# Where a loop's exponentials and gate products are queued

## The chip, the cores and the metric

The kernel runs on one core of a Trainium2 chip. The metric is the device time of one execution in microseconds; times inside an execution are counted from the start of the profiled span. The engines are named as the profile names them: PE (TensorE matmul), PEld (its weight loads), DVE (VectorE), ACT (ScalarE), POOL (GpSimd), SP (SyncE, which here only issues transfers). Each works through its own queue in order.

## The reference

One layer over 512 tokens of width 1024: a gated spatial mix and a banded attention, both projected and added to the input, and then a feed-forward part with 16384 experts, which is where the change lies. Cut to that part:

```python
def block(xb):                                   # 128 tokens
    q = (xb @ w_query).reshape(128, 8, 2, 128)   # 8 heads, 2 halves
    sc = einsum('thpd,hpkd->thpk', q, sub_keys)
    s_top, i_top = lax.top_k(sc, 16)
    cand = s_top[:, :, 0, :, None] + s_top[:, :, 1, None, :]
    cand_idx = i_top[:, :, 0, :, None] * 128 + i_top[:, :, 1, None, :]
    best, pos = lax.top_k(cand.reshape(128, 8, 256), 16)
    eidx = take_along_axis(cand_idx.reshape(128, 8, 256), pos, axis=-1)
    g = softmax(best, axis=-1)
    h = gelu(einsum('thkd,td->thk', expert_u[eidx], xb))
    return einsum('thk,thkd->td', g * h, expert_v[eidx])
```

## The kernel before, in words

The 512 tokens are four tiles of 128. For 320 tokens (and 64 further ones that are handled on the side) the expert part is computed densely: all 16384 experts in 128 tiles of 128, as `gelu(U x)` times a gate that is zero for experts that were not chosen, and then times `V`. For the first tile of 128 tokens it is computed by gathering: 16 rows of `U` and 16 of `V` for each of 8 heads.

The loop at the end of the kernel runs over 64 chunks of two expert tiles. The **first product** (PE, L194 to L196, into one of two PSUM buffers `pu`) makes `U x`; a **gelu** on ACT (L719) moves it to `act` and so frees the buffer. The **second product** (L1202) multiplies by `V` and adds to PSUM. The first products run 25 chunks ahead of the second ones (`AHEAD`): 50 gelus lie ahead of the loop, and in chunk c the loop does second product c and, while c + 25 < 64, the first products and two gelus of chunk c + 25. So the first 39 chunks hold both products and the last 25 only the second.

For each chunk the second product needs: two tiles of `V` (a transfer to `raw`, a copy to `hi` on ACT, L155, and a difference `lo`, L156, mostly on DVE); `act` times the gates `gc` (two DVE products, L1168); the copy `wh` of that on ACT (L1169) and the difference `wl` on DVE (L1170), each in one of two buffers. The gates are loaded (L1002) for groups of eight expert tiles, which is four chunks (`GB // BC`), into two buffers in turn, one group ahead.

The gathered tile's heads are **routed** in the loop, one every third chunk (`ROUTE`), by `route_gathered`: the best keys (DVE), the casts L762 and L763 (ACT), the choice (DVE, with one copy on POOL), and the **softmax**: a subtraction (L803, DVE), an exponential (L804, ACT), a sum, a reciprocal and a product (L806 to L808, DVE). Rows are then gathered by POOL; DVE multiplies each row of `U` with the tokens (L1128), ACT takes the gelu of 16 such results (L1132), DVE multiplies them with the head's softmax (L1133) and adds each row of `V` with that weight (L1139).

Only PE's order is written out by hand in the loop. The other engines' queues are ordered by a planner, which starts from the order in the program, priorities (the second products and the first products ahead have a raised one) and the times at which it expects inputs. `queued_behind(marks)` and `tc.issue_after(ins)` add one constraint: an instruction of the block that runs on the engine of `ins` comes behind `ins` in that engine's queue. It adds no wait. `done` holds the last gelu, `marked` the last `wl` difference (and, before the loop, the last instruction of that kind of work on DVE).

Of the kernel before, what the change touches and what calls it, by code (L numbers as in the profile page):

```python
# [13 lines left out]
AF = mybir.ActivationFunctionType  # L14
# [5 lines left out]
P = 128  # L20
# [7 lines left out]
TOPK = 16  # L28
# [23 lines left out]
BC = 2  # L52
# [26 lines left out]
PARTS = 8  # L79
ROUTE = 3  # L80
GB = 8
# [12 lines left out]
def hybrid_block(tc, x, ln1, w_in, gng, wsT, bsb, qkg, bias, w_out, ln2, wq, skT, uT, ud, vd, out):  # L94
    nc = tc.nc
    ctx = ExitStack()
    with ctx:
# [28 lines left out]
        def queued_behind(marks):  # L126

            ctx = ExitStack()
            for i in marks:
                ctx.enter_context(tc.issue_after(i))  # L130
            return ctx
# [557 lines left out]
        begun, more, done, behind, routed = [], [], [], [], []  # L689
# [51 lines left out]
        def keys(pool, n):  # L741

            return (pool.tile([P, 2, n, 2, TOPK], F32, name="top", tag="top", bufs=2),
                    pool.tile([P, n, 2, TOPK], U32, name="pos", tag="pos", bufs=2))

        def best_keys(pool, top, pos, u, p2, src):
            rep = pool.tile([P, NK], F32, name="rep", tag="rep", bufs=2)
            return top16(top[:, 0, u, p2, :], pos[:, u, p2, :], src, rep)
# [47 lines left out]
                                          mask[:, i, :, :, None].to_broadcast([P, n, TOPK, m]), other)  # L796
            nc.vector.tensor_copy(to, tree[:, :, :, 0])

        def softmax(pool, best, n):

            full = [P, n, TOPK]
            ex = pool.tile(full, F32, name="ex")
            nc.vector.tensor_tensor(ex, best, best[:, :, 0:1].to_broadcast(full), op=ALU.subtract)  # L803
            nc.scalar.activation(ex, ex, AF.Exp)  # L804
            zs = pool.tile([P, n], F32, name="zs")
            nc.vector.reduce_sum(zs, ex, axis=AX.X)  # L806
            nc.vector.reciprocal(zs, zs)
            nc.vector.tensor_tensor(best, ex, zs[:, :, None].to_broadcast(full), op=ALU.mult)  # L808
# [186 lines left out]
        gcs, marked = {}, []  # L995
# [20 lines left out]
        with tc.manual_schedule(engines=engines):  # L1016
# [5 lines left out]
            for n in range(steps + LEAD):  # L1022
                t, c = divmod(n, per)
# [65 lines left out]
        ep = ctx.enter_context(tc.tile_pool(name="ep", bufs=1, reuse_waits="tile"))  # L1089
        gcp.append(ep)  # L1090

        def scores_of(b, eng):
            n = NH // PARTS
            sc = ep.tile([P, n, 2, NK], F32, name="sc0", tag="sc0", bufs=2)
            load = eng.dma_start(sc.rearrange("p h a n -> p h (a n)"),
                                 s0d[b * n:(b + 1) * n].rearrange("h p a -> p h a"))
            return sc, getattr(load, "ins", load)
# [9 lines left out]
        def route_gathered(b):  # L1107

            n = NH // PARTS
            sc = (scores.pop(b) if b in scores else scores_of(b, nc.sync))[0]  # L1110
            top, pos = keys(ep, n)
            for h in range(n):
                for p2 in range(2):
                    best_keys(ep, top, pos, h, p2, sc[:, h, p2, :])
            hs = slice(b * n * TOPK, (b + 1) * n * TOPK)
            best, to = (x[:, 0, hs].rearrange("p (h k) -> p h k", k=TOPK) for x in (gate, eidx))
            mask = ep.tile([P, 6 * n * TOPK], U32, name="mask", tag="mask", bufs=1)
            tree = ep.tile([P, D], F32, name="tree", tag="row", bufs=ROW)
            choose(ep, pairs(ep, top, pos, n, behind=list(routed if b else done)), n, best, to, mask,
                   tree[:, 0:n * TOPK * 32].rearrange("p (h k m) -> p h k m", h=n, k=TOPK))  # L1120
            softmax(ep, best, n)
            nc.vector.tensor_copy(eint[:, hs], eidx[:, 0, hs])

        def gather_u(j):
            row = ep.tile([P, D], F32, name="row", tag="row", bufs=ROW)
            nc.gpsimd.indirect_dma_start(out=row, out_offset=None, in_=ud,  # L1126
                                         in_offset=bass.IndirectOffsetOnAxis(ap=eint[:, j:j + 1], axis=0))
            nc.vector.scalar_tensor_tensor(row, row, 1.0, xb0, op0=ALU.mult, op1=ALU.mult,  # L1128
                                           accum_out=hw[:, j:j + 1])
            if j % TOPK == TOPK - 1:  # L1130
                hs = slice(j + 1 - TOPK, j + 1)
                nc.scalar.activation(hw[:, hs], hw[:, hs], AF.Gelu_apprx_tanh)  # L1132
                nc.vector.tensor_tensor(hw[:, hs], hw[:, hs], gate[:, 0, hs], op=ALU.mult)  # L1133
# [24 lines left out]
        def second_product(c, between):  # L1158
            w = weights.pop(c) if c in weights else rows_of_v(c)
            gc = gcs[c * BC // GB]  # L1160
            act = acts.pop(c)
            wh = ep.tile([P, BC, NDT], F32R, name="wh", tag="wh", bufs=2)
            wl = ep.tile([P, BC, NDT], F32R, name="wl", tag="wl", bufs=2)
            with queued_behind(marked if c < GB // BC else []):
                for b in range(BC):
                    bb = (c * BC + b) % GB
                    av = act[:, b, :].rearrange("p (n t) -> p n t", t=TG)
                    nc.vector.tensor_tensor(av, av, gc[:, 0:NDU // TG, bb, :], op=ALU.mult)  # L1168
            nc.scalar.activation(wh[:, :, 0:NDU], act, AF.Copy)  # L1169
            mark = nc.vector.tensor_tensor(wl[:, :, 0:NDU], act, wh[:, :, 0:NDU].bitcast(F32), op=ALU.subtract)  # L1170
            marked[:] = [getattr(mark, "ins", mark)]
            if c == 1:
                with tc.issue_after(loads[-1]):
                    load_gates(1, nc.sync)
            elif c * BC % GB == 0 and 0 < c * BC < NB - GB:
                load_gates(c * BC // GB + 1, nc.sync)
            b0 = (c * BC) % GB

            def last_tokens():
                gu = gc[:, NDU // TG:, b0:b0 + BC, :]  # L1180
                hu, lu = (w_[:, :, NDU:].rearrange("p b (n t) -> p n b t", t=TG) for w_ in (wh, wl))
                pair = (nc.scalar.activation(hu, gu, AF.Copy),
                        nc.vector.tensor_tensor(lu, gu, hu.bitcast(F32), op=ALU.subtract))
                own_last[:] = [getattr(i, "ins", i) for i in pair]

            if c:
                with queued_behind(own_last if c < GB // BC else []):
                    last_tokens()
            order = [(b, t) for b in range(BC) for t in range(ND)]
            if c in (0, NCHK - 1):  # L1190
                order.sort(key=lambda bt: bt[1])
            for i, (b, t) in enumerate(order):
                if c == 0 and i == BC * (ND - 1):
                    between()
                    with queued_behind(halved):
                        last_tokens()
                first = c == 0 and b == 0
                last = c == NCHK - 1 and b == BC - 1
                tok = slice(t * P, (t + 1) * P)
                def product(half, k):  # L1200
                    ds_ = slice(half * 512, (half + 1) * 512)
                    nc.tensor.matmul(accs[t][half], (wh, wh, wl)[k][:, b, tok], w[b][k % 2][:, ds_],  # L1202
                                     start=first and k == 0, stop=last and k == 2)

                if c == NCHK - 1:
                    parts = [(half, k) for half in range(2) for k in range(3)]
                else:
                    parts = [(half, k) for half in range(2) for k in range(2)] + [(0, 2), (1, 2)]
                for half, k in parts:
                    product(half, k)  # L1210
            return mark
# [3 lines left out]
        with tc.manual_schedule(engines={mybir.EngineType.PE}):  # L1215
            for c in range(NCHK):
                def ahead():
                    if c + AHEAD < NCHK:
                        for _ in first_products((c + AHEAD) * BC, BC):
                            pass  # L1220

                with tc.high_priority(offset=PRIO):
                    mark = second_product(c, ahead)
                    if c:
                        ahead()
                if c % ROUTE == 0 and c < PARTS * ROUTE:
                    route_gathered(c // ROUTE)
                passed = c + 1 + min(c + 1, NCHK - AHEAD)
                with tc.issue_after(mark.ins if hasattr(mark, "ins") else mark):
                    gather_some(min(total, total * max(0, passed - DELAY) // (weight - SLACK - DELAY))  # L1230
                                - (total - len(gathers)))
            gather_some(len(gathers))
# [53 lines left out]
```

## Time and profile before

| | |
|---|---|
| median of 3 runs | 1425.32 us (1420.27 to 1426.73) |
| the profiled execution | 1418.47 us |
| its span | 1416.7 us |
| mean granted PE clock | 0.998 |
| PE busy | 1387.3 us, 98% of the span |
| DVE busy | 1157.5 us, 82% |
| ACT busy | 610.5 us, 43% |
| POOL busy | 699.0 us, 49% |

A busy share is a mean over stages. The loop begins at about 585 us; its first 39 chunks end at about 1212 us, and a chunk there takes 15.3 us of PE, later 8.2 us. In the profile's rows an instruction has its start, its duration, engine, line, operation, and what it writes and reads; a bracket behind it gives the time its engine stood idle before it and what ended that.

### The profile page before, as it was taken

To read this page: it belongs to the slowest core of one execution; us is meant where nothing else is said; L and a number is where in the kernel's file an instruction comes from. 1 tells how busy PE (TensorE), PEld (TensorE's weight loads), DVE (VectorE), ACT (ScalarE), POOL (GpSimd) and SP (SyncE) were. 2 spreads that over 40 slices of the span, in tenths; PEclk is the share of its full clock that TensorE was granted. 3 is DMA by queue.
4 is the path that set the end of the run, shared out by engine and by line. 5 is a ranking of instruction groups with operands and counts; after the bars stand their busy time and mean duration, and the time that the engine had idled before them with its cause. 6 is when DMAs were issued, how large, how long until landed. Compare 5 with 4: busy or idle time off the path is not lost.

```text
span 1416.7 us, 21660 instructions
## 1 busy us (share of the span) xinstructions
PE 1387.3 (98%) x7838; PEld 1224.6 (86%) x7838; DVE 1157.5 (82%) x2505; ACT 610.5 (43%) x955; POOL 699.0 (49%) x486
## 2 busy tenths in 40 slices
PE   9999999999998999989999999999999999999998
PEld 7887788899998989978998889889889989888877
DVE  5537845898999998679999999889989887688883
ACT  5447635443443545444434443334433334333331
POOL 0002104778779898325554556455565553345430
PEclk9999999999999999999999999999999999999999
DMA  4452326667667999978999899999999998888882
GB/s 165 133 193 75 105 75 193 209 214 275 235 229 257 330 352 272 292 265 332 334 331 356 328 352 347 355 376 353 386 375 365 347 364 311 288 332 326 335 335 89
DMA packets 164330, 396.24 MB, mean 280 GB/s; under 512 B 12880, under 2 KB 75232, under 8 KB 162176
## 3 DMA queue, kind: packets, MB, share of 16 engines
q1 hardware_dynamic: 64640, 194.14, 37.9%
q0 software_dynamic: 48176, 173.46, 33.2%
q10 hardware_dynamic: 51408, 27.27, 6.5%
q8 instruction: 61, 1.00, 0.3%
q14 instruction: 45, 0.37, 0.1%
HBM read 363.34 MB, written 31.46 MB: 279 GB/s over the span
## 4 chain that ended last, share of the span: by engine, by line
PE 31%; DVE 12%; DMA 8%; issue 4%; ACT 1%; POOL 0%; SPq 0%; DVEq 0%; ACTq 0%; POOLq 0%
PE pa L1202 13%; PE px L1202 6%; PE pu L194 4%; PE pu L196 4%; PE pu L195 4%; DMA gc<-gd 4%; DVE lo L156 3%; DVE row L1128 2%; DVE acc L1139 2%; DMA row<-in_ud,eint 2%; DVE act L1168 1%; DMA raw<-in_uT 1%; DMA row<-in_vd,eint 1%; DVE wl L1170 1%; DMA raw<-in_vd 1%
## 5 line engine op out<-in xcount | busy, mean ns | idle before, releaser
L155 ACT ACTIVATE hi<-raw 128x1024 fp32r<-128x1024 f32 x296 | 312.9, 1059 | 470.9 <-DMA raw<-in_vd 156.6
L156 DVE TENSOR_TENSOR lo<-raw,hi 128x1024 fp32r<-128x1024 f32 x244 | 307.0, 1259 | 72.1 <-ACT hi L155 71.6
L1126 POOL DMA_INDIRECT row<-in_ud,eint x128 | 198.5, 1551 | 159.6 <-DVE acc L1139 107.2
L1137 POOL DMA_INDIRECT row<-in_vd,eint x128 | 179.7, 1404 | 192.0 <-DVE row L1128 131.5
L194 PE MATMUL pu<-xch,hi 128*128 128x320 f32 x784 | 247.5, 316 | 8.6 <-ACT act L719 8.6
L196 PE MATMUL pu<-xch,lo 128*128 128x320 f32 x784 | 242.8, 310 | 0.0
L195 PE MATMUL pu<-xcl,hi 128*128 128x320 f32 x784 | 242.7, 310 | 0.0
L1202 PE MATMUL pa<-lo,wh 128*128 128x512 f32 x512 | 199.7, 390 | 0.0
L1202 PE MATMUL pa<-hi,wh 128*128 128x512 f32 x512 | 199.4, 389 | 0.0
L156 POOL TENSOR_TENSOR lo<-raw,hi 128x1024 fp32r<-128x1024 f32 x52 | 124.1, 2401 | 116.3 <-ACT hi L155 115.3
L1139 DVE SCALAR_TENSOR_TENSOR acc<-row,hw,acc 128x1024 f32<-128x1024 f32 x128 | 165.6, 1294 | 2.4 <-DMA row<-in_vd,eint 2.0
L1128 DVE SCALAR_TENSOR_TENSOR row<-row,xb 128x1024 f32<-128x1024 f32 x128 | 155.9, 1220 | 12.0 <-DMA row<-in_ud,eint 12.0
L1202 PE MATMUL pa<-hi,wl 128*128 128x512 f32 x512 | 158.4, 389 | 0.0
L194 PEld LDWEIGHTS pu<-xch,hi 128*128 128x128 f32 x784 | 148.0, 189 | 12.0 <-ACT act L719 10.4
L195 PEld LDWEIGHTS pu<-xcl,hi 128*128 128x128 f32 x784 | 148.1, 189 | 1.4
L196 PEld LDWEIGHTS pu<-xch,lo 128*128 128x128 f32 x784 | 147.8, 188 | 0.2 <-DVE lo L156 0.2
L1202 PEld LDWEIGHTS pa<-hi,wh 128*128 128x128 f32 x512 | 96.1, 188 | 20.6
L1202 PEld LDWEIGHTS pa<-hi,wl 128*128 128x128 f32 x512 | 96.1, 188 | 20.2
L1202 PEld LDWEIGHTS pa<-lo,wh 128*128 128x128 f32 x512 | 96.1, 188 | 20.2
L985 PE MATMUL pa<-bm,am 128*128 128x128 f32 x768 | 96.3, 279 | 7.9 <-DVE am L976 5.0
L985 PEld LDWEIGHTS pa<-bm,am 128*128 128x128 f32 x768 | 92.3, 194 | 10.8 <-issue 5.5
L1202 PE MATMUL px<-hi,wh 128*128 128x512 f32 x256 | 100.1, 391 | 0.6 <-ACT hi L155 0.6
(236 smaller groups left out, 2634.1 us busy)
## 6 DMA issues: line engine op xcount, KB each, us to landing
raw<-in_uT SPq DMA_DIRECT2D x128, 512.0 KB, 5.6
raw<-in_vd SPq DMA_DIRECT2D x128, 512.0 KB, 6.1
gd<-gst ACTq DMA_DIRECT2D x24, 1024.0 KB, 8.9
gc<-gd SPq DMA_DIRECT2D x15, 1280.0 KB, 9.8
raw<-in_w_in SPq DMA_DIRECT2D x19, 512.0 KB, 4.6
raw<-in_wq SPq DMA_DIRECT2D x16, 512.0 KB, 4.5
raw<-in_w_out SPq DMA_DIRECT2D x8, 512.0 KB, 3.7
gc<-gd SPq DMA_DIRECT2D x15, 256.0 KB, 10.3
```

The costliest lines, as they stand in the source:

```text
L155: top = nc.scalar.activation(hi, raw, AF.Copy)
L156: ins = eng.tensor_tensor(lo, raw, hi.bitcast(F32), op=ALU.subtract)
L194: nc.tensor.matmul(ps, lh[0], rh[0], start=first, stop=False)
L195: nc.tensor.matmul(ps, lh[0], rh[1], start=False, stop=False)
L196: nc.tensor.matmul(ps, lh[1], rh[0], start=False, stop=last)
L985: nc.tensor.matmul(ps[:, i * P:(i + 1) * P], am[:, 4 * q + i, :], bm[:, 4 * q + i, :], start=True, stop=True)
L1126: nc.gpsimd.indirect_dma_start(out=row, out_offset=None, in_=ud, in_offset=bass.IndirectOffsetOnAxis(ap=eint[:, j:j + 1], axis=0))
L1128: nc.vector.scalar_tensor_tensor(row, row, 1.0, xb0, op0=ALU.mult, op1=ALU.mult, accum_out=hw[:, j:j + 1])
L1137: nc.gpsimd.indirect_dma_start(out=row, out_offset=None, in_=vd, in_offset=bass.IndirectOffsetOnAxis(ap=eint[:, j:j + 1], axis=0))
L1139: nc.vector.scalar_tensor_tensor(acc0, row, hw[:, j:j + 1], acc0, op0=ALU.mult, op1=ALU.add)
L1168: nc.vector.tensor_tensor(av, av, gc[:, 0:NDU // TG, bb, :], op=ALU.mult)
L1202: nc.tensor.matmul(accs[t][half], (wh, wh, wl)[k][:, b, tok], w[b][k % 2][:, ds_], start=first and k == 0, stop=last and k == 2)
```

## The change

Two things are moved; no instruction of the computation is added or taken away.

The softmax of a routed head is cut in two. The subtraction stays in `route_gathered` (new function `shifted`), behind the conversion of the indices. The rest, from the exponential on, is written two chunks later, at the end of chunk 3b + 2 for head b, and the exponential is queued behind `done`, the second gelu that this chunk issued.

The products of `act` with the gates were queued behind `marked`, the `wl` of the chunk ahead, in the first four chunks only; now they are in every chunk.

```diff
-        def softmax(pool, best, n):
+        def shifted(pool, best, n):
 
             full = [P, n, TOPK]
             ex = pool.tile(full, F32, name="ex")
             nc.vector.tensor_tensor(ex, best, best[:, :, 0:1].to_broadcast(full), op=ALU.subtract)
-            nc.scalar.activation(ex, ex, AF.Exp)
+            return ex
+
+        def softmax(pool, best, n, ex=None, behind=()):
+
+            full = [P, n, TOPK]
+            if ex is None:
+                ex = shifted(pool, best, n)
+            with queued_behind(behind):
+                nc.scalar.activation(ex, ex, AF.Exp)
             zs = pool.tile([P, n], F32, name="zs")
...
-            softmax(ep, best, n)
             nc.vector.tensor_copy(eint[:, hs], eidx[:, 0, hs])
+            return best, n, shifted(ep, best, n)
...
-            with queued_behind(marked if c < GB // BC else []):
+            with queued_behind(marked):
                 for b in range(BC):
...
                 if c % ROUTE == 0 and c < PARTS * ROUTE:
-                    route_gathered(c // ROUTE)
+                    chosen = route_gathered(c // ROUTE)
+                if c % ROUTE == ROUTE - 1 and c < PARTS * ROUTE:
+                    softmax(ep, *chosen, behind=list(done))
```

## The prediction

> **What bounds the kernel now.** I read the page's busy shares first, then the table of windows, then the list of waits, and then the timelines of the few places where TensorE stands.
>
> ```profile
> PE 1387.3 (98%) x7838; PEld 1224.6 (86%) x7838; DVE 1157.5 (82%) x2505; ACT 610.5 (43%) x955; POOL 699.0 (49%) x486
> ```
> ```profile
> core 0: us, PE busy (x) PEld busy (x) DVE busy (x) ACT busy (x) POOL busy (x), PEclk, DMA share, GB/s
> 640.00:760.00 120.00, 119.22 (x660) 107.75 (x659) 117.28 (x302) 54.52 (x82) 65.70 (x45) 1.00 0.90 330
> 760.00:880.00 120.00, 116.95 (x634) 104.34 (x633) 113.96 (x210) 50.67 (x73) 65.55 (x47) 1.00 0.93 346
> ...
> 1212.00:1357.00 145.00, 143.36 (x633) 118.44 (x632) 119.22 (x162) 51.81 (x72) 63.60 (x43) 1.00 0.85 318
> ```
> ```profile
> 631.70:635.50 3.80, 3.78 (x16) 3.78 (x17) 0.03 (x1) 0.30 (x1) 1.62 (x2) 0.57 1.00 414
> ```
>
> PE is the bound: 98% busy over the span. So a change in the loop can win only the time in which PE stands or runs at a lower clock there. VectorE is close behind it between 640 and 880 us: 231.2 of 240 us busy. ACT is not full (105 of 240 us), but its queue is in order, and the waits tell where that bites:
>
> ```profile
> DVE act L1168 <- DMA gc<-gd: 40.3, 12, 5.3
> ...
> ACT ex L804 <- DVE ex L803: 12.3, 5, 4.2
> ...
> PE pu L194 <- ACT act L719: 8.6, 4, 4.7
> ```
>
> The third row is what the change can reach first: four times PE waits for a gelu (L719) to free one of the two `pu` buffers. The PE timeline shows those four places and a fifth one, late, where the weights `wl` were not there:
>
> ```profile
> 626.55 0.31 PE L195 MATMUL pu<-xcl,hi 128*128 128x320 f32 x1
> 626.70 0.31 PE L196 MATMUL pu<-xch,lo 128*128 128x320 f32 x1
> 631.72 0.41 PE L194 MATMUL pu<-xch,hi 128*128 128x320 f32 x1 [4.71 <-ACT act L719]
> ...
> 751.51 0.61 PE L1202 MATMUL pa<-hi,wl 128*128 128x512 f32 x2
> 752.91 0.42 PE L194 MATMUL pu<-xch,hi 128*128 128x320 f32 x1 [0.78 <-ACT act L719]
> ...
> 798.53 0.61 PE L1202 MATMUL pa<-hi,wl 128*128 128x512 f32 x2
> 800.07 0.41 PE L194 MATMUL pu<-xch,hi 128*128 128x320 f32 x1 [0.92 <-ACT act L719]
> ...
> 845.50 0.61 PE L1202 MATMUL pa<-hi,wl 128*128 128x512 f32 x2
> 848.25 0.41 PE L194 MATMUL pu<-xch,hi 128*128 128x320 f32 x1 [2.13 <-ACT act L719]
> ...
> 1353.89 0.39 PE L1202 MATMUL px<-hi,wh 128*128 128x512 f32 x1
> 1354.12 0.39 PE L1202 MATMUL px<-lo,wh 128*128 128x512 f32 x1
> 1356.15 0.73 PE L1202 MATMUL px<-hi,wl 128*128 128x512 f32 x2 [1.64 <-DVE wl L1170]
> ```
>
> Matmuls overlap, so I count from start to start: a 320-column one takes 0.15 (626.55 to 626.70), a 512-column one 0.23 (1353.89 to 1354.12). Above that the five stalls cost 4.87, 0.94, 1.08, 2.29 and 1.80 us, together 10.98. Behind the long one the granted clock is 0.57 for 3.80 us (the window 631.7 to 635.5), which loses 3.80 x 0.43 = 1.63 more; the short ones left it at 1.00. All that stands in reach is 12.6 us.
>
> **The change part by part.** First the exponential. What ACT did before two of the stalls:
>
> ```profile
> 624.37 0.29 ACT L1182 ACTIVATE wh<-gc 128x128 fp32r<-128x128 f32 x1
> 627.81 0.21 ACT L804 ACTIVATE ex<-ex 128x16 f32<-128x16 f32 x1 [3.15 <-DVE ex L803]
> 627.93 1.99 ACT L155 ACTIVATE hi<-raw 128x1024 fp32r<-128x1024 f32 x2
> 629.94 1.28 ACT L719 ACT_TABLE_LOAD   x1
> 631.23 0.77 ACT L719 ACTIVATE act<-pu 128x320 f32<-128x320 f32 x2
> ...
> 842.29 1.28 ACT L804 ACT_TABLE_LOAD   x1
> ...
> 845.38 1.06 ACT L155 ACTIVATE hi<-raw 128x1024 fp32r<-128x1024 f32 x1 [1.58 <-DMA raw<-in_uT]
> 846.46 1.28 ACT L719 ACT_TABLE_LOAD   x1
> ```
>
> An Exp in front of a gelu costs a table load, itself, and a load back: 1.28 + 0.21 + 1.28 = 2.77 us, plus any wait for the subtraction (L803) that feeds it, with copies and gelus queued behind. Taken away, stall by stall:
> - 626.7: the two copies follow at 624.66, take 1.99, and the first gelu (0.44, half of two rows' worth) ends at 627.1; PE resumes 0.4 late. If one copy then waits for its load, as the copy at 845.38 did for 1.58, it is 2.0 late. I take 1.0, nearer the end whose rows are of this place. Won: 4.87 - 1.0 + 1.63 (an idle stretch that short leaves the clock) = 5.5, with ends 4.5 and 6.1.
> - 751.5 and 798.5: lateness 0.94 and 1.08, less than the 2.77 that goes. Won: 2.02.
> - 845.5: the copy at 845.38 waits for its DMA in any case and ends at 846.44; the gelu then ends at 846.88 instead of 848.19. Won: 1.31; all 2.29 if that load comes earlier because VectorE is less in arrears. I take 1.31, the row as it stands.
>
> Sum of the first part: 8.8 us.
>
> What comes in its place. Exp of head b now stands behind the second gelu that chunk 3b+2 issues. 50 gelus come before the loop's own, so for head 0 this is gelu 56:
>
> ```profile
> L719 ACT ACTIVATE act<-pu x56: 415/423/445, 224.4 to 653.8; 128x320 f32<-128x320 f32 x56
> ```
> ```profile
> L804 ACT ACTIVATE ex<-ex x8: 215/216/218, 621.5 to 843.6; 128x16 f32<-128x16 f32 x8
> L804 ACT ACT_TABLE_LOAD  x7: 1283/1283/1283, 620.2 to 842.3; - x7
> ```
> ```profile
> L1133 DVE TENSOR_TENSOR hw<-hw,gate x8: 153/163/203, 677.4 to 1330.5; 128x16 f32<-128x16 f32 x8
> ```
>
> So head 0's Exp moves from 621.5 to some 654 us, and each later head's by three chunks from there. Its first user, the product with the gates (L1133), is at 677.4: 23 us remain, and heads are used further apart (eight over 653 us, 93 each) than they are routed (some 46), so nobody waits for a gate. Its input is ready two chunks earlier, so the 12.3 us of ACT waiting for L803 go. The Exp issues no DMA and passes none on SP's or POOL's queue. Behind it on ACT stand copies and the next chunk's first gelu, which now gets the 2.77 us. The room it has is from the gelu's end to PE's first matmul that needs that buffer; the narrowest two of the new places, in the trace of before, are:
>
> ```profile
> 718.72 0.42 ACT L719 ACTIVATE act<-pu 128x320 f32<-128x320 f32 x1
> ...
> 813.66 0.42 ACT L719 ACTIVATE act<-pu 128x320 f32<-128x320 f32 x1
> ```
> ```profile
> 721.43 0.31 PE L194 MATMUL pu<-xch,hi 128*128 128x320 f32 x1
> ```
> ```profile
> 815.42 0.31 PE L194 MATMUL pu<-xch,hi 128*128 128x320 f32 x1
> ```
>
> That is 2.29 and 1.34 us. If the load to Exp's table and the Exp fall into ACT's waits for loads and only the load back delays the gelu, 1.28 fits into both: cost 0. If all 2.77 comes on top, 0.48 and 1.43 are lost: 1.9. Heads 0 and 1 also shared one load pair (seven loads for eight Exps: one at 620.2 served 621.5 and 627.8) and no longer do; that pair lies at 654 to 704, where ACT is 45% busy. I take 0.7 us lost, nearer 0, because the earlier Exps that made these very gelus late are gone too.
>
> The Trainium skill, "ScalarE: Activation LUTs", section on table sets, speaks against this part: calls should be batched by set, and it prices each switch at about 2.66 us, 1.28 of load and 1.38 of drain. The trace has the load (846.46, 1.28) starting 0.02 us after the copy before it ends: no drain to be seen, so I keep 2.77 for the pair. By the page's price it would be an estimated 5.5 us per head, some 3 and 4 us lost at the two narrow places, and the whole would come out near a gain of 4 us instead of 10.
>
> Second, the scaling by gates. Before, all eight products of a group of four chunks were put into VectorE's queue at once, at the time the planner expected the gates, up to three chunks before use:
>
> ```profile
> 1349.71 2.10 DVE L1168 TENSOR_TENSOR act<-act,gc 128x320 f32<-128x320 f32 x5 [5.31 <-DMA gc<-gd]
> ...
> 1355.27 0.82 DVE L1170 TENSOR_TENSOR wl<-act,wh 128x640 fp32r<-128x640 f32 x1
> ```
> ```profile
> gc<-gd SPq DMA_DIRECT2D x15, 1280.0 KB, 9.8
> ```
>
> VectorE stood 5.31 us for gates, did 3.4 us of products, and only then the `wl` that PE wanted at 1354.35. With each chunk's two products behind the `wl` of the chunk ahead, six of the eight leave this place and the group's first pair comes two to three chunks after the gates' load is issued (16 us or more, where such a load takes 9.8, the last row). The 1.80 us stall goes; lower end 0, if the copy (L1169) is what is late. I take 1.80. The 128 products themselves stay. Each pair must now be done between `wl` of the chunk ahead and its own copy, one PE chunk (8.2 us late in the loop) later; it takes 0.9 us. Cost 0, covered by that chunk; with the cover gone, each microsecond of lateness beyond it would be PE's. No load moves: gates are still released by the last tokens' copies (L1182, L1183), so SP's queue stands as it did.
>
> Sum: 8.8 + 1.8 - 0.7 = 9.9 us off the profiled 1418.47 gives 1408.6. That execution is 6.85 us under the median of the runs; off the median 1425.32 it is 1415.4.
>
> **The rivals.**
> - *The switch only changes its gelu.* VectorE's arrears, not the Exp, make ACT late between 700 and 880 us, and with PE no longer stalling they grow by the 4.3 us that the three short stalls gave it; the pair then lands on gelus with no room. For: VectorE has 8.8 us idle there in 240. Against: gelus without an Exp in front never stalled PE here. Four heads at 2.77 less some 1 us of room each lose 7, and 10.6 - 7 = 3.6 won: about 1421.7, within 0.5%.
> - *VectorE stands for the Exp* (slower). The sum of the exponentials (L806) is in VectorE's in-order queue, with the row products and splits behind. Before, VectorE never waited there. Now the Exp waits for a gelu that itself runs 8 us or so behind PE, and if the planner puts L806 right behind the time it believes, VectorE stands for the difference. Five heads between 640 and 880 at 6 us are 30; its 8.8 idle and about 2 us of room per stall in ACT take up some 13, 17 reach PE, against 10 won: +7 to +9, about 1433. It decides from some 4.5 us per head. Against: VectorE is itself late there, so it comes to L806 after ACT.
> - *The products come too late.* Late in the loop the chain `wl`, two products, copy, `wl` takes 0.8 + 0.9 + 0.7 + 0.8 = 3.2 of 8.2 us; two splits or row products (1.2 each) ahead at each step would bring it to 8. Only the 1.8 would then be lost: 1417, still the forecast's side.
>
> **How the numbers follow.** Within 0.5% (7.1 us) is what a measurement of this kernel can't tell from no change; the forecast lies 2.8 us beyond it. Forecast 0.62, of which 0.60 beyond 0.5% and 0.02 short of it; the switch on another gelu 0.26, all within; VectorE standing 0.12, of which 0.10 beyond and 0.02 within. So faster 0.60, same 0.30, slower 0.10. The runs shown spread from 1420.3 to 1426.7. Low end: 1420.3 less the whole 12.6 is 1408. High end: the first rival with the upper run, 1426.7 - 1 or 2 us, is 1425. Outside are the slower case and little else.
>
> **What would show it.** Right: the PE timeline has no wait of 4 us near 626 and no clock under 1.00 behind it; the wait list's gelu row falls from 8.6 to under 2; VectorE's wait for `gc` falls from 40.3 to about 9 (the loop's first two groups remain); Exps run from about 650 to 985 us, each with its own load pair, 8 and 8. Wrong: new waits of PE on L719 right after the Exps' new places, a row in which VectorE's L806 waits for ACT's L804, or PE waiting for `wl` more than once.

## The result, and the profile after

The changed kernel takes 1412.53 us (median of 10 runs, 1411.15 to 1415.20), the kernel before 1419.97 us on the same chip (10 runs, 1416.26 to 1426.73). The medians differ by 7.4 us, 0.5%. The ratio, which is taken over the runs and not from the two medians, is 0.9940, with a 95% interval from 0.9925 to 0.9955. One execution of the variant e7 below, 1707.8 us at a mean granted clock of 0.752, is left out of its median and its ratio. The profiled execution of the changed kernel took 1411.74 us, its span is 1410.0 us, 6.7 us below the span before. Line numbers have moved: Exp is L812 now, the sum behind it L814, the products with the gates L1176, `wh` L1177, `wl` L1178, the second product L1210, the row product L1136.

The page's busy shares, then the same three windows as before (busy time and count of PE, PEld, DVE, ACT, POOL; clock; DMA share; GB/s):

```profile
PE 1387.7 (98%) x7838; PEld 1226.5 (87%) x7838; DVE 1156.4 (82%) x2505; ACT 612.5 (43%) x957; POOL 670.8 (48%) x486
```
```profile
640.00:760.00 120.00, 119.85 (x663) 108.26 (x662) 117.56 (x300) 48.75 (x75) 64.17 (x45) 1.00 0.91 330
760.00:880.00 120.00, 118.36 (x652) 106.66 (x651) 117.66 (x214) 55.06 (x78) 62.66 (x49) 1.00 0.96 363
1212.00:1357.00 145.00, 145.00 (x642) 120.09 (x641) 132.17 (x176) 51.68 (x72) 65.44 (x48) 1.00 0.93 342
```

PE gains in all three, and late in the loop it no longer stands at all (145.00 of 145). VectorE is fuller than before between 640 and 880 us: 235.2 of 240 us, where it was 231.2.

The waits of the loop (engine and instruction that waited, what it waited for: us in all, times, longest):

```profile
ACT top L762 <- DVE pos L739: 31.5, 5, 8.5
...
DVE act L1176 <- DMA gc<-gd: 4.7, 1, 4.7
PE pu L194 <- ACT act L719: 4.1, 4, 2.3
...
DVE zs L814 <- ACT ex L812: 1.1, 3, 0.6
```

VectorE's standing for gates fell from 40.3 to 4.7 us, and there is no row for Exp waiting for its subtraction (12.3 before). In its place ACT's longest wait of this kind is a cast (L762) waiting for VectorE's search (L739), 31.5 us, where it was 17.1. PE's waits for a gelu halved, from 8.6 to 4.1. They lie here (PE timeline):

```profile
626.74 0.31 PE L196 MATMUL pu<-xch,lo 128*128 128x320 f32 x1
629.35 0.41 PE L194 MATMUL pu<-xch,hi 128*128 128x320 f32 x1 [2.30 <-ACT act L719]
...
718.58 0.61 PE L1210 MATMUL pa<-hi,wl 128*128 128x512 f32 x2
719.35 0.41 PE L194 MATMUL pu<-xch,hi 128*128 128x320 f32 x1 [0.15 <-ACT act L719]
...
764.76 0.61 PE L1210 MATMUL pa<-hi,wl 128*128 128x512 f32 x2
766.53 0.42 PE L194 MATMUL pu<-xch,hi 128*128 128x320 f32 x1 [1.16 <-ACT act L719]
...
770.01 0.31 PE L196 MATMUL pu<-xch,lo 128*128 128x320 f32 x1
770.80 0.41 PE L194 MATMUL pu<-xch,hi 128*128 128x320 f32 x1 [0.48 <-ACT act L719]
```

From start to start, less what such matmuls take (0.15 or 0.23), these are 2.46, 0.32, 1.32 and 0.64 us. The three at 751, 798 and 845 and the one at 1354 are gone. Behind the first one the granted clock halved, as it had before (windows of the changed kernel: PE busy, clock, DMA share, GB/s):

```profile
629.35:630.60 1.25, 1.25 (x8) 1.00 1.02 315
630.60:633.80 3.20, 3.20 (x14) 0.50 0.99 413
```

The first stall is still there for this reason (ACT's timeline, with an earlier copy of the same kind in its first row, then a row of PE's):

```profile
607.09 1.06 ACT L155 ACTIVATE hi<-raw 128x1024 fp32r<-128x1024 f32 x1 [3.73 <-PE pu L195]
...
624.41 0.29 ACT L1190 ACTIVATE wh<-gc 128x128 fp32r<-128x128 f32 x1
626.97 2.00 ACT L155 ACTIVATE hi<-raw 128x1024 fp32r<-128x1024 f32 x2 [2.27 <-issue]
628.88 0.75 ACT L719 ACTIVATE act<-pu 128x320 f32<-128x320 f32 x2
```
```profile
626.59 0.31 PE L195 MATMUL pu<-xcl,hi 128*128 128x320 f32 x1
```

The Exp no longer stands ahead of the two copies, but they waited 2.27 us themselves, and the gelu stands behind both. For this wait the profile names nothing ("issue"). The times point to PE: a copy needs one of the five `hi` buffers, and L195 is the last to read one. The first copy starts 0.38 us after the start of PE's last L195 in this kernel and in e1, e3, e6 and e9 below, and in all five PE's stall is 2.46 us. The copy at 607.09, for which the profile does name L195, starts 0.35 us after one (606.74). The load of its input was not what it waited for, at least in e1: the two loads there were issued at 618.3 and 621.6 and took 3.5 to 4.4 us, so the first of them was there by 622.7, and the copy that reads it started at 626.09.

The stall at 766.53, on ACT:

```profile
752.77 0.22 ACT L812 ACTIVATE ex<-ex 128x16 f32<-128x16 f32 x1
752.89 1.04 ACT L155 ACTIVATE hi<-raw 128x1024 fp32r<-128x1024 f32 x1
761.19 0.22 ACT L762 ACTIVATE top<-pos 128x16 f32<-128x16 uint32 x1 [7.26 <-DVE pos L739]
...
763.67 1.06 ACT L155 ACTIVATE hi<-raw 128x1024 fp32r<-128x1024 f32 x1 [0.40 <-DMA raw<-in_uT]
764.75 1.28 ACT L719 ACT_TABLE_LOAD   x1
766.04 0.44 ACT L719 ACTIVATE act<-pu 128x320 f32<-128x320 f32 x1
```

The load back to gelu's table is the last thing before the gelu, but ACT had just stood 7.26 us in front of a cast. Whether the load or the wait counts is what the experiments had to tell.

### The profile page after: what moved, and what is told of

Read it like the earlier page. It is cut to its first block, busy times and chain, and to the rows that moved or that the text cites. A ratio compares the mean times of both kernels' runs of the same rounds, so it can differ in the third digit from the quotient of the medians.

```text
span 1410.0 us, 21681 instructions
## 1 busy us (share of the span) xinstructions
PE 1387.7 (98%) x7838; PEld 1226.5 (87%) x7838; DVE 1156.4 (82%) x2505; ACT 612.5 (43%) x957; POOL 670.8 (48%) x486
## 4 chain that ended last, share of the span: by engine, by line
PE 46%; DVE 5%; DMA 3%; issue 1%; ACT 0%; POOL 0%; POOLq 0%; ACTq 0%; DVEq 0%
PE pa L1210 20%; PE px L1210 10%; PE pu L194 5%; PE pu L196 5%; PE pu L195 5%; DVE lo L156 2%; DVE row L1136 1%; DMA row<-in_vd,eint 1%; DMA row<-in_ud,eint 1%; DMA raw<-in_vd 1%; DMA raw<-in_uT 1%; DVE acc L1147 1%; DVE act L1176 0%; DVE rep L737 0%; ACT hi L155 0%
## 5 line engine op out<-in xcount | busy, mean ns | idle before, releaser
L1134 POOL DMA_INDIRECT row<-in_ud,eint x128 | 192.6, 1505 | 184.4 <-DVE acc L1147 131.3
L1145 POOL DMA_INDIRECT row<-in_vd,eint x128 | 158.4, 1237 | 178.8 <-DVE row L1136 117.5
L195 PE MATMUL pu<-xcl,hi 128*128 128x320 f32 x784 | 243.1, 310 | 0.0
L1210 PE MATMUL pa<-lo,wh 128*128 128x512 f32 x512 | 199.7, 390 | 0.0
L1210 PE MATMUL pa<-hi,wh 128*128 128x512 f32 x512 | 199.3, 389 | 0.0
L1136 DVE SCALAR_TENSOR_TENSOR row<-row,xb 128x1024 f32<-128x1024 f32 x128 | 155.7, 1220 | 9.1 <-DMA row<-in_ud,eint 9.1
L1210 PE MATMUL pa<-hi,wl 128*128 128x512 f32 x512 | 158.4, 389 | 0.0
L195 PEld LDWEIGHTS pu<-xcl,hi 128*128 128x128 f32 x784 | 148.3, 189 | 1.4
L1210 PEld LDWEIGHTS pa<-hi,wh 128*128 128x128 f32 x512 | 96.1, 188 | 20.5
L1210 PEld LDWEIGHTS pa<-lo,wh 128*128 128x128 f32 x512 | 96.1, 188 | 20.2
L1210 PEld LDWEIGHTS pa<-hi,wl 128*128 128x128 f32 x512 | 96.1, 188 | 20.2
L1210 PE MATMUL px<-hi,wh 128*128 128x512 f32 x256 | 100.1, 391 | 0.2 <-ACT hi L155 0.2
```

The source lines that it names most:

```text
L195: nc.tensor.matmul(ps, lh[0], rh[1], start=False, stop=False)
L1145: nc.gpsimd.indirect_dma_start(out=row, out_offset=None, in_=vd, in_offset=bass.IndirectOffsetOnAxis(ap=eint[:, j:j + 1], axis=0))
```

## The experiments

Each is a variant of the changed kernel unless it says otherwise, and each ratio is to the kernel before on the same chip. The kernels ran 4 to 12 times each. "Stalls" are places where PE's start-to-start time exceeds the usual by more than 0.3 us, in the loop from 600 us on of the one profiled execution; time lost to a lower clock behind them is not in the sum.

| kernel | median, us | before, us | ratio (95%) | stalls, us |
|---|---|---|---|---|
| changed | 1412.53 | 1419.97 | 0.9940 (0.9925 to 0.9955) | 4.7 |
| e1 Exp's place alone | 1421.54 | 1420.41 | 1.0003 (0.9991 to 1.0015) | 13.5 |
| e2 products' place alone | 1417.37 | 1420.41 | 0.9970 (0.9958 to 0.9981) | 7.9 |
| e3 no table switch | 1412.23 | 1420.41 | 0.9937 (0.9921 to 0.9952) | 5.8 |
| e4 Exp in the same chunk | 1412.78 | 1420.41 | 0.9940 (0.9927 to 0.9953) | 5.7 |
| e5 casts on VectorE | 1413.72 | 1420.03 | 0.9940 (0.9924 to 0.9957) | 5.1 |
| e6 e1 with half row products | 1416.96 | 1420.03 | 0.9976 (0.9965 to 0.9987) | 8.7 |
| e7 before with half row products | 1413.91 | 1420.03 | 0.9948 (0.9932 to 0.9964) | 6.7 |
| e8 routing a chunk later | 1426.61 | 1420.03 | 1.0042 (1.0027 to 1.0057) | 14.4 |
| e9 casts on VectorE from head 2 | 1414.34 | 1421.09 | 0.9946 (0.9930 to 0.9963) | 6.4 |
| e10 e2 with e9's casts | 1416.67 | 1421.09 | 0.9957 (0.9940 to 0.9973) | 10.8 |

For the kernel before the stalls are 11.0.

**e1, Exp's place alone.** The products' part is undone.

```diff
-            with queued_behind(marked):
+            with queued_behind(marked if c < GB // BC else []):
```

> The exponential's part alone: the products with the gates are queued behind the weights of the chunk ahead in the first four chunks only, as before the change. Theory (two separate gains): PE's short waits for a gelu near 751 and 798 us are gone and the one near 845 is smaller or gone, but the late wait of PE for wl near 1350 us stays at about 1.8 us and VectorE still waits some 40 us in all for gc; time 3 to 5 us under the kernel before, 2 to 4 over the changed one. Rival A (it was all the products): time as before, within 1 us. Rival B (the exponential is all of it): time as the changed kernel.

Measured: no gain. The stalls at 751, 798 and 845 are gone and others stand in their place. The waits, and VectorE's and PE's timelines at the worst of them:

```profile
DVE act L1176 <- DMA gc<-gd: 42.5, 12, 5.5
```
```profile
711.95 1.70 DVE L1176 TENSOR_TENSOR act<-act,gc 128x320 f32<-128x320 f32 x4 [2.47 <-DMA gc<-gd]
713.56 1.22 DVE L156 TENSOR_TENSOR lo<-raw,hi 128x1024 fp32r<-128x1024 f32 x1
714.70 1.69 DVE L1176 TENSOR_TENSOR act<-act,gc 128x320 f32<-128x320 f32 x4
```
```profile
713.02 0.39 PE L1210 MATMUL px<-hi,wh 128*128 128x512 f32 x1
714.84 0.50 PE L1210 MATMUL px<-lo,wh 128*128 128x512 f32 x1 [1.43 <-DVE lo L156]
...
718.37 0.61 PE L1210 MATMUL pa<-hi,wl 128*128 128x512 f32 x2
721.88 0.41 PE L194 MATMUL pu<-xch,hi 128*128 128x320 f32 x1 [2.90 <-ACT act L719]
```

VectorE stood 2.47 us for gates with a split queued behind, did four products, then the split that PE wanted, then four more. PE stood 1.59 us for that split and 3.06 for a gelu behind it. Behind the second of them the granted clock was 0.67 for 4.5 us. With the Exp out of the way ACT no longer loses the time in front of it, but VectorE still does.

**e2, the products' place alone.** The softmax is in one piece again, as before.

```diff
+            softmax(ep, best, n)
             nc.vector.tensor_copy(eint[:, hs], eidx[:, 0, hs])
-            return best, n, shifted(ep, best, n)
...
-                    chosen = route_gathered(c // ROUTE)
-                if c % ROUTE == ROUTE - 1 and c < PARTS * ROUTE:
-                    softmax(ep, *chosen, behind=list(done))
+                    route_gathered(c // ROUTE)
```

> The products' part alone: the softmax stays in one piece in the routing, as before the change. Theory: VectorE's wait for gc falls from 40.3 to about 5 to 9 us and the late wait of PE for wl is gone, but PE's waits for a gelu near 626, 751 and 798 us stay (8 to 10 us in all, with the half clock behind the first); time 1.5 to 3 us under the kernel before. Rival A (it was all the products): time as the changed kernel, 7 us under. Rival B: time as before.

Measured: 0.3% faster. The late stall is gone (e1 still has it, 2.04 us), and stalls for gelus remain, 3.60, 2.98 and 1.35 us. Its waits:

```profile
ACT ex L812 <- DVE ex L803: 12.8, 3, 5.8
...
PE pu L194 <- ACT act L719: 7.5, 3, 3.4
```

So the two parts are not a sum. Alone they give 0.0 and 0.3%, together 0.6%: in medians, the Exp's place wins 4.8 us (1417.37 to 1412.53) where the products are moved, and nothing where they are not. The remaining runs ask why.

**e3, no table switch.** `AF.Copy`, which here came without a table load, stands in for Exp in the routed heads.

```diff
-                nc.scalar.activation(ex, ex, AF.Exp)
+                nc.scalar.activation(ex, ex, AF.Copy if pool is not rq else AF.Exp)
```

> The changed kernel with a plain copy in place of the routed heads' exponential, so that ACT loads no other table for them (the exponential of the first tile's softmax is left out). Theory: the two table loads are what remains of the change's cost, PE's new waits near 719 and 766 to 771 us (2.3 us together) are gone and the wait near 626 us stays, since no exponential is near it any more; time 2 us under the changed kernel. Rival (the casts' waits for VectorE's positions make those waits by themselves): the waits near 766 stay at 1 us or more and the time is the changed kernel's.

Measured: 1412.23 us, no difference from the changed kernel that these runs could tell; a gain of 2 us lies at the edge of what the two intervals exclude. Sixteen table loads of 1.28 us are gone (957 instructions on ACT become 941). PE's stalls, in the slowest of its six runs, are 2.46, 2.03 and 1.31: the one that followed the load at 764.75 is gone, and those near 719 and 771 are longer than in the changed kernel (0.32 and 0.64). By its waits ACT stands in front of the casts as it did:

```profile
ACT top L762 <- DVE pos L739: 33.5, 6, 8.9
...
PE pu L194 <- ACT act L719: 5.3, 3, 2.3
```

The load at 764.75 was last in the chain, but taking the loads away didn't take the stalls away.

**e4, Exp in the same chunk.** Still behind a gelu, but at the end of the chunk that routes the head.

```diff
-                if c % ROUTE == ROUTE - 1 and c < PARTS * ROUTE:
+                if c % ROUTE == 0 and c < PARTS * ROUTE:
```

> The changed kernel with the rest of the softmax written at the end of the same chunk as its routing (3b instead of 3b + 2), still behind that chunk's second gelu. Theory (the two chunks matter, because the subtraction comes late on VectorE): ACT again waits for L803, 5 us or more in all, and PE waits for gelus for 3 us or more beyond the changed kernel; time 2 to 6 us over the changed one. Rival (any place behind a gelu will do): ACT's wait for L803 under 1 us and the time is the changed kernel's within 1 us.

Measured: 1412.78 us, the same. No Exp waits for its subtraction in the list. What pays is the order behind a gelu; the two chunks add nothing that can be measured in the time. They do keep head 0's Exp clear of the first stall: here its load back stands ahead of the gelu, and that stall is 3.61 us instead of 2.46.

**e5, casts on VectorE.** The casts L762 and L763 leave ACT, and with them the constraint on their place.

```diff
-            choose(ep, pairs(ep, top, pos, n, behind=list(routed if b else done)), n, best, to, mask,
+            choose(ep, pairs(ep, top, pos, n, own=True), n, best, to, mask,
```

> The changed kernel with the routed heads' two casts (L762, L763) on VectorE instead of ACT. Theory (what remains of PE's waits near 719 and 766 to 771 us comes from ACT standing for VectorE's positions, 42 us in all, not from the table switch): those waits go, the one near 626 us may stay, time 2 to 4 us under the changed kernel. Rival (VectorE's arrears set them, and 16 more small instructions add to these): PE's waits stay at 2 us or more and the time is the changed kernel's or above.

Measured: 1413.72 us. After 640 us no stall over 0.3 us is left, but the first one doubled to 5.14 us, with the clock at 0.53 from 633 to 638. ACT's timeline there:

```profile
625.63 1.06 ACT L155 ACTIVATE hi<-raw 128x1024 fp32r<-128x1024 f32 x1 [5.98 <-DMA raw<-in_vd]
...
631.53 1.06 ACT L155 ACTIVATE hi<-raw 128x1024 fp32r<-128x1024 f32 x1 [2.12 <-DMA raw<-in_uT]
632.49 0.75 ACT L719 ACTIVATE act<-pu 128x320 f32<-128x320 f32 x2
```

Without the casts as a brake the planner routed the first heads earlier (the first subtraction is at 604.0 instead of 620.6 us, and POOL gathers rows from 609.5 instead of 628.3 us), and the copies of V and U waited 5.98 and 2.12 us for loads. The gain moved, and it was lost at one place.

**e6 and e7, relief for VectorE.** The row product is done over half of its 1024 columns and the rest is left out: e6 is e1 with that edit, e7 is the kernel before with it.

```diff
-            nc.vector.scalar_tensor_tensor(row, row, 1.0, xb0, op0=ALU.mult, op1=ALU.mult,
-                                           accum_out=hw[:, j:j + 1])
+            nc.vector.scalar_tensor_tensor(row[:, 0:512], row[:, 0:512], 1.0, xb0[:, 0:512], op0=ALU.mult,
+                                           op1=ALU.mult, accum_out=hw[:, j:j + 1])
```

> The exponential's part alone, with VectorE's product of each gathered row of U made over half of its 1024 columns (the other half is left out), which takes some 0.5 us off each of 128 instructions. Theory (VectorE's arrears between 640 and 880 us decide whether a late exponential, a late gate load or a late score load reaches PE): PE's stalls there fall from 11 us and more to under 3, time 6 to 10 us under the same kernel with whole rows. Rival (the order of the queues alone makes the stalls): 5 us or more of them stay and the time moves by less than 3.

> The kernel before, with the product of each gathered row of U made over half of its columns (the other half is left out). Theory (VectorE's arrears): PE's waits near 751, 798 and 845 us (4.3 us) go although the exponentials stand where they stood, the one near 626 us, where no row has been gathered yet, stays with its half clock; time 4 to 7 us under the kernel before. Rival (an exponential ahead of a gelu makes them by itself): two or more of the three stay and the time is 0 to 3 us under.

Measured: VectorE's busy time between 640 and 880 us falls to 209.3 (e6) and 211.7 (e7). In e7 the stalls at 751, 798, 845 and 1354 are gone, and behind 640 us 1.6 us of stalls are left, where there were 6.1. The Exps are still queued ahead of gelus and waited even longer (e7's waits):

```profile
DVE act L1168 <- DMA gc<-gd: 41.8, 15, 4.8
ACT ex L804 <- DVE ex L803: 25.6, 6, 6.6
...
PE pu L194 <- ACT act L719: 5.8, 3, 4.9
```

So with VectorE relieved these waits cost PE little there. But the Exps don't stand at the same times: those of heads 2 to 7 come 5 to 48 us earlier than in the kernel before (the last at 822.3 instead of 843.6), so that the relief alone did it, and not their new places, isn't shown. In e6 the loss fell by 4.6 us against e1, but PE waited for gelus four times, 8.0 us, two of them near 675 and 680 us, where e1 has no stall; VectorE stood 38.6 us for gates and casts waited up to 9.5 us (e6's waits):

```profile
DVE act L1176 <- DMA gc<-gd: 38.6, 15, 4.6
ACT top L763 <- DVE pos L739: 28.6, 6, 9.5
...
PE pu L194 <- ACT act L719: 8.0, 4, 2.5
```

Arrears explain part of e1, then, not all. In this pair the Exp's move even costs 3.0 us (1413.91 to 1416.96).

**e8, routing a chunk later.** This tests the place of the stall near 626 us.

```diff
-                if c % ROUTE == 0 and c < PARTS * ROUTE:
+                if c % ROUTE == 1 and c < PARTS * ROUTE:
```

> The changed kernel with every head's routing written one chunk later (3b + 1 instead of 3b; the rest of the softmax stays at 3b + 2). Theory (PE's wait near 626 us, 2.5 us and 1.5 more at the half clock, comes from the routing of the first two heads ahead of the splits on VectorE): it goes and the time is 2 to 4 us under the changed kernel. Rival (it only moves with the routing, or it is the load of the raw tile itself): a wait of 2 us or more stays between 620 and 650 us and the time is the changed kernel's within 1.5 us.

Measured: slower by 0.4%, which neither side expected. The first stall fell to 1.24 us with the clock at 1.00 behind it. The copies wait as before (1.99 us), but now only one stands ahead of the first gelu (ACT's timeline):

```profile
627.58 1.06 ACT L155 ACTIVATE hi<-raw 128x1024 fp32r<-128x1024 f32 x1 [1.99 <-issue]
628.54 0.42 ACT L719 ACTIVATE act<-pu 128x320 f32<-128x320 f32 x1
```

So what ACT's queue holds between that wait and the gelu sets the length of this stall: 1.24 us with one copy (e8), 2.46 with two (the changed kernel, e1, e3, e6, e9), 3.60 or 3.61 with two and a table load (e2, e4, e10). Elsewhere it got worse: PE stalls ten times between 705 and 916 us, for gelus and for splits. That this comes from routing falling together with the gathered rows is a guess. PE is idle for 6.7 us of this window alone (columns as above):

```profile
760.00:880.00 120.00, 113.33 (x605) 100.47 (x604) 116.74 (x276) 51.50 (x76) 59.80 (x45) 0.99 0.94 347
```

**e9 and e10, casts on VectorE from head 2 on.** e9 is the changed kernel, e10 is e2, each with

```diff
-            choose(ep, pairs(ep, top, pos, n, behind=list(routed if b else done)), n, best, to, mask,
+            choose(ep, pairs(ep, top, pos, n, own=b > 1, behind=list(routed if b else done)), n, best, to, mask,
```

> The changed kernel with the two casts on VectorE from head 2 on; heads 0 and 1 keep them on ACT, queued as in the changed kernel. Theory (what is left of the change's stalls has two causes: ACT standing for the casts' input after 640 us, and the first heads' routing ahead of the splits near 626 us): PE's waits near 719 and 766 to 771 go as they did with all casts on VectorE, the wait near 626 stays as in the changed kernel (2.5 us, 4 with the half clock) instead of growing to 5; time 1.5 to 3 us under the changed kernel. Rival (without the casts as a brake the planner pulls heads 2 and 3 ahead and the wait near 626 grows anyway): 5 us there and the time of the changed kernel.

> The products' part alone (exponential at its old place) with the two casts on VectorE from head 2 on. Theory (an exponential at its old place makes ACT stand for L803, and that alone reaches PE once VectorE no longer stands for gates): ACT's wait for L803 stays at 5 us or more, PE waits for gelus 2 to 4 us beyond the same kernel with the exponential moved, time 2 to 4 us over that one. Rival (only ACT's standing in all counts, and the casts were most of it): the two kernels agree within 1 us.

Measured: e9 1414.34, e10 1416.67 us. In e9 ACT has no row of waiting for L739 any more, and PE still stalls at 716.9, 749.7, 757.5, 766.1 and 797.7 us, 4.0 us together. The casts' waits are therefore not the cause, or not alone, of what remained in the changed kernel; the stalls at 749.7 and 757.5 are waits for VectorE's split `lo`. Between e9 and e10 only the Exp's place differs (e9's waits, then e10's):

```profile
PE pu L194 <- ACT act L719: 4.5, 4, 2.3
```
```profile
ACT ex L812 <- DVE ex L803: 14.1, 4, 4.5
...
PE pu L194 <- ACT act L719: 9.8, 6, 3.5
```

PE's waits for gelus double and the median is 2.3 us higher, though the two intervals overlap.

**What the runs give together.** In the stage from 640 to 880 us VectorE is nearly as full as PE, and an instruction at the head of an in-order queue that waits for something (VectorE for gates, ACT for Exp's input or a cast's) pushes back what PE needs next. Moving the products takes 36 us of VectorE's standing away, and with that the late stall. Moving the Exp takes ACT's standing for L803 away; by e1 and e2 this reaches PE only where the products are moved too, and e1's timeline shows how at its worst place: PE waits there for VectorE's splits, and for a gelu behind them, instead. No variant was measurably faster than the changed kernel. What stays open is why e6 keeps 6.2 us of stalls after 640 us with VectorE relieved; the planner's order differs between e6 and e7, and no run separated that from the Exp's place. Nor was a gelu put ahead of the two copies near 627 us, or a further `hi` buffer given, with everything else left as it is.

## Why the prediction was right or wrong, point by point

The time came out 2.9 us below the 1415.4 of the forecast's sum and inside the range. Part of that agreement is luck: the saving was forecast at 9.9 us and measured at 6.7 in the spans and 7.4 in the medians, but it was taken off a median of 1425.32 from three runs, where ten give 1419.97.

| step | predicted, us | measured, us |
|---|---|---|
| stall at 626.7, with its half clock | 5.5 won (4.5 to 6.1) | 2.4 won |
| stalls at 751 and 798 | 2.02 won | 2.02 won |
| stall at 845 | 1.31 won (up to 2.29) | 2.29 won |
| stall for `wl` at 1354 | 1.80 won | 1.80 won |
| new lateness of gelus | 0.7 lost (0 to 1.9) | 2.3 lost |
| sum | 9.9 | 6.2 |

The measured column is worked out from the PE timelines; the 0.5 us to the spans' 6.7 is mostly a stall for a copy `hi` near 594 us, which fell from 0.75 to 0.38.

- **The term that was mis-sized is the first.** I let the copies follow at 624.66 without a gap, or with one of 1.58 for a load, and took 1.0 us of lateness. With the Exp gone they still started at 626.97 only, with PE's last product of the tile, and the gelu came behind both. So PE stood 2.46 us more than usual and the clock halved, which I had excluded for a shorter stretch. Both ends of that term were too good: 2.4 us came, of 5.5. A row of the waits of the kernel before says what such copies wait for besides loads:

```profile
ACT hi L155 <- PE pu L195: 62.1, 27, 5.1
```

- **The late stall** went as told. It is there in e1 and gone in e2, so the products' place is enough for that; in e7 it went without.
- **The stall at 845** went entirely. I had named that end, "if that load comes earlier because VectorE is less in arrears", and not taken it. The condition came true and the reason isn't shown: the copies there have their loads by 839.69 and 842.88 us, and the gelu is done before the Exp at 845.58, but VectorE is fuller between 640 and 880 us than before.
- **The new lateness** exceeded its end of 1.9. I priced the table switch alone; in e3, without switches, the stalls behind 640 us are not shorter (3.3 us against 2.3).
- **The waits of VectorE for Exp** (the slower rival) are 1.1 us in three, so that rival fell. The products never came too late: PE has no wait for `wl` left.
- **The rival that the switch only changes its gelu** came true in small: there are new stalls between 700 and 880 us, 2.3 us where it priced 7. Whether the switches, the casts' waits or both carry them the runs leave open: without switches (e3) they stay, without casts on ACT (e5) they go, but the first stall doubles.
- **The signs** named beforehand are mixed. No wait of 4 us is left near 626 us, gates fell below the 9 us named, and the Exps have eight loads. But the clock there was 0.50, the row of waits for gelus fell to 4.1 and not under 2, and two signs of being wrong came in small: PE's new waits for gelus, 14 to 18 us behind an Exp, and VectorE's for Exp.
- **The unstated assumption** was that the parts add up. They don't: e1 alone wins nothing. The sum came out near because both halves were made together.

The Exps stand where the forecast put them, each with a load of its own (first and last start, in the loop):

```profile
L812 ACT ACT_TABLE_LOAD  x8: 1283/1283/1283, 655.1 to 979.4; - x8
L812 ACT ACTIVATE ex<-ex x8: 215/216/217, 656.4 to 980.7; 128x16 f32<-128x16 f32 x8
```

"ScalarE: Activation LUTs" of the Trainium skill, in its section on table sets, speaks for batching calls by set. This kernel now has one more pair of switches than before and is faster, and e3 has none and is no faster still: ACT is 43% busy here, and by e4 it was the Exp's place in the queue that paid.

## What to carry to other kernels

Where a second engine is nearly as full as the first, the gains of two moves need not add: find the waits at the head of the queue on every engine that feeds the bound one, and try the moves together as well as alone. The last instruction of a chain (here a table load) need not be its cause; an experiment that takes it away tells cheaply. When a stall is to go by taking one instruction out of a queue, ask what those left ahead of the wanted one wait for themselves, here copies that start with the bound engine's own last product, and price the stall by that.

## What the runs showed of the hardware

A stall of the same length at the same place can halve the clock or not. After 2.61 us from start to start (626.74 to 629.35) the changed kernel ran at 0.50 for 3.20 us, beginning 1.25 us after PE had resumed. After the same 2.46 us of excess the clock was 1.00 in e3 (its window behind the stall, all columns):

```profile
631.20:635.70 4.50, 4.50 (x28) 4.37 (x29) 2.49 (x4) 0.25 (x1) 3.93 (x2) 1.00 1.00 394
```

and in e1 and e9 too (1.00 in the 4.5 us behind it), while in e6 it was 0.62 in the 4.5 us behind it. Over the stalls of all twelve traces, counted as above, an excess of up to 1.79 us never lowered the clock in the 4.5 us behind it, one of 2.62 us or more did every time (to a mean of 0.50 to 0.67), and of the fourteen between 1.91 and 2.46 us four did. The traces don't show what decides among these. "TensorE: Matmul & The Clock Gate" of the Trainium skill, in the section on the clock gate, describes a free-running window of about 3.4 us and a halved clock after one idle window. That the place in such a window counts would fit these rows; that a whole idle one is needed doesn't, since PE stood for 2.30 us here and for 1.75 us at the shortest of the four (e1, 756.21). One such stretch costs about 1.6 us (3.20 times 0.50).

Sixteen table loads fewer made no difference in time that these runs could tell, and each load was seen as 1283 ns, with the gelu starting right behind the one at 764.75 (plus 1.28, then 766.04).
